# Twelve of 31 convolution taps split between ScalarE and VectorE in a two-layer decoder trunk

## The chip, the cores and the metric

The program runs on one core of a Trainium2 chip. The metric is the device time of one execution in microseconds (us), lower is better. The engines work side by side, each through its own queue in order: TensorE (PE, its weight loads PEld), VectorE (DVE), ScalarE (ACT), GpSimd (POOL) and SyncE (SP), which issues the DMAs here.

## What is computed

Two layers over 256 tokens of width 1024. Each has a gated mixing sublayer of three branches (a convolution module, differential attention, block-sparse attention) that are merged with sigmoid gates and projected by `w_o`, a layer norm, an MLP of width 4096 with squared ReLU, and another layer norm. The part that the change touches is the depthwise causal convolution of 31 taps over 512 channels:

```python
def conv_branch(u, conv_w, conv_b, ln_g, ln_b, w_out):
    a, gt = jnp.split(u, 2, axis=-1)
    h = a * jax.nn.sigmoid(gt)
    h = lax.conv_general_dilated(h, conv_w, window_strides=(1,), padding=[(30, 0)],
        dimension_numbers=("NWC", "WIO", "NWC"), feature_group_count=512) + conv_b
    h = jax.nn.silu(layer_norm(h, ln_g, ln_b))
    return h @ w_out

def reference(x, ...):
    for l in range(2):
        u = x @ w_in[l]
        u_conv, dq, dk, dv, mq, mk, mv, g = jnp.split(u, offs, axis=-1)
        y_a = conv_branch(u_conv, ...)
        y_b = diff_attention(dq, dk, dv, ...)      # rotary on q and k, two softmaxes, subtracted
        y_c = moba_attention(mq, mk, mv, ...)      # rotary on q and k, causal softmax
        gates = jax.nn.sigmoid(g + b_gate[l]).reshape(B, S, 3, D)
        m = gates[:, :, 0] * y_a + gates[:, :, 1] * y_b + gates[:, :, 2] * y_c
        x = layer_norm(alpha * x + m @ w_o[l], ...)
        h = jnp.square(jax.nn.relu(x @ w_ff1[l] + b_ff1[l]))
        x = layer_norm(alpha * x + h @ w_ff2[l] + b_ff2[l], ...)
    return x
```

## The kernel before

**Precision and weights.** Every large matmul is made of three (`mm3`, line 400): the operands are split into a rounded high half and a low half, and high times high, low times high and high times low are added in PSUM. `Weights.get` (line 348) fetches a unit of 128x1024 by DMA into `raw` (a ring of four), ScalarE casts the high half `whi`, VectorE subtracts to get the low half `wlo`; both halves have rings of eight. `split` (line 390) does the same for activations.

**Order of the work.** Nothing is issued where it is written. `Plan.record` (line 111) collects all operations with their dependences. `Plan.latest` (line 185) goes backwards through them and gives each a latest start. `Plan.order` (line 239) then walks forward with a cost for each operation and, on each engine, takes among the operations that are ready the one whose latest start is earliest; a tile whose ring has no free buffer isn't ready. The result fixes the order in each engine's queue; the chip runs each queue in that order. So an operation without an early due time goes where its engine has nothing more urgent that is ready, and a change in one place can reorder the queues elsewhere.

**The convolution.** The gated projection is transposed into `hpad`, four channel groups of 128 channels (partitions) by 30 zeros and 256 tokens (lines 596 to 635). `tap(c, k)` (line 600) is one instruction of VectorE over 128x256: for k = 0 it writes `acc[:, c]` as product plus bias, for k > 0 it adds `hpad` shifted by k, times the tap's weight, one number a partition, to `acc[:, c]`. All 124 taps of a layer are on VectorE (lines 636 to 640); `R.bias` shifts their due time by `CONV_BIAS`, which is 0. `acc` is read much later, by the transposes of `conv_ln` (line 825) while the third set of gates is computed.

**Around it.** TensorE goes on with the two value projections (line 643), the q and k projections with `rope` (lines 657 and 816), which writes each rotated unit into a tile `qk` from a ring of seven, and the attention, whose steps are hung on a counter of weight units (`tick`, line 590): `attn_scores` (line 674) reads two `qk` tiles on TensorE, then VectorE and ScalarE make the softmax, and `d_a` to `d_d` or `m_a` to `m_c` finish each head. `m_a` (line 772) multiplies the weights of a head by one number a partition on ScalarE with `AF.Copy`. Then come `gates` and `outs` (lines 873 and 888): in `outs` VectorE multiplies the projected branch by its gate, adds it to the sum `macc`, and for the last branch splits the sum into `M`, the operand of the projection by `w_o` (line 926). There, on TensorE, the first high times high matmuls are followed by one with the low half of the first piece of `M`. Layer norm, MLP and the next layer follow.

Of the kernel before, what the change touches and what calls it, by code (L numbers as in the profile page):

```python
# [9 lines left out]
F32 = mybir.dt.float32  # L10
F32R = mybir.dt.float32r
AF = mybir.ActivationFunctionType
ALU = mybir.AluOpType

P = 128
D = 1024
SEQ = 256
# [3 lines left out]
TAPS = 31  # L21
# [3 lines left out]
RAWS = 4  # L25
WARM = 5
NW = 8
CONV_BIAS = 0
GATED = (("gate", 0), ("out", 0), ("gate", 1), ("gate", 2), ("out", 1), ("out", 2))
BANKS = {"pm": 2, "pa": 4, "pt": 2}  # L30

# [2 lines left out]
C_CW = 24  # L34
# [332 lines left out]
def kernel(ctx: ExitStack, tc: tile.TileContext, x, xT, w_in, w_p2, w_o, w_f1, w_f2,  # L367
# [7 lines left out]
    work = ctx.enter_context(tc.tile_pool(name="work", bufs=2))  # L375
# [3 lines left out]
    R = Plan(nc)  # L379
# [4 lines left out]
    def slot(dtype=F32R, name="b"):  # L384
        return R.tile(big, [P, 1024], dtype, "big", NSLOT)
# [79 lines left out]
    for (c0, _), (c1, _) in zip(pieces, pieces[1:]):  # L465
        k, n = c0 // 256 % 2, (c1 - c0) // 256
# [11 lines left out]
    for l in range(L):  # L478
        c = R.tile(const, [P, NCOL], F32, f"cols{l}", 1)
# [3 lines left out]
    for t in range(NT):  # L483
        a = slot(F32, "xtok")
# [48 lines left out]
    for l in range(L):  # L533
# [17 lines left out]
        half = R.tile(const, [P, NCOL], F32, f"half{l}", 1)  # L551
# [25 lines left out]
        def qkunit():  # L577
            ps = bank()
            for c in range(2):
                w = W.get(k=KT)  # L580
                for kt in range(KT):
                    mm3(ps[:, c * 256:(c + 1) * 256], at(w, ALLP, kt), x_at(X, kt), kt == 0,
                        kt == KT - 1)
                tick()
            return ps
# [10 lines left out]
        hpad = R.tile(work, [P, 4, TAPS - 1 + SEQ], F32, "hpad", 1)  # L596
        acc = slot(F32, "acc").rearrange("p (c n) -> p c n", c=4)
        R.Pool.memset(hpad[:, :, 0:TAPS - 1], 0.0)

        def tap(c, k):  # L600
            wcol = half[:, C_CW + c * TAPS + k:C_CW + c * TAPS + k + 1]
            src = hpad[:, c, k:k + SEQ]
            if k == 0:
                R.DVE.tensor_scalar(acc[:, c], src, wcol, C[:, C_CB + c:C_CB + c + 1],
                                        op0=ALU.mult, op1=ALU.add)
            else:
                R.DVE.scalar_tensor_tensor(acc[:, c], in0=src, scalar=wcol, in1=acc[:, c],
                                               op0=ALU.mult, op1=ALU.add)
# [25 lines left out]
            o = TAPS - 1 + t * P  # L634
            R.Activation.copy(hpad[:, :, o:o + P], ps.rearrange("p (c n) -> p c n", c=4))
        for c in range(4):
            for k in range(TAPS):
                R.bias = CONV_BIAS
                tap(c, k)
                R.bias = 0.0  # L640


        wv = [W.get(k=2) for _ in range(8)]
# [13 lines left out]
        def rope(ps, dst):  # L657
            qq = R.tile(work, [P, 1024], F32, "zz", 3)
            q, qr = qq[:, :512], qq[:, 512:]
            p3 = ps.rearrange("p (c n) -> p c n", c=2)  # L660
            q3 = q.rearrange("p (c n) -> p c n", c=2)
            qr3 = qr.rearrange("p (c n) -> p c n", c=2)
            d3 = dst.rearrange("p (c n) -> p c n", c=2)
            cb = cosT.rearrange("p (o n) -> p o n", o=1).broadcast_to([P, 2, SEQ])
            R.DVE.tensor_mul(q3, p3, cb)
            for c in range(2):
                R.DVE.tensor_mul(qr3[:, c], p3[:, 1 - c], sinT)
            R.DVE.tensor_sub(d3[:, 0], q3[:, 0], qr3[:, 0])
            R.DVE.tensor_add(d3[:, 1], q3[:, 1], qr3[:, 1])
# [146 lines left out]
        for b in range(2):  # L816
            for u in range(2):
                for w in 'qk':
                    ps = qkunit()
                    d = R.tile(work, [P, 512], F32, "qk", 7)  # L820
                    rope(ps, d)
                    QK[b, w, u] = d.rearrange("p (c n) -> p c n", c=2)

# [136 lines left out]
        for t in range(NT):  # L960
            for c in range(2):
                n, nk = ((512, 2), (256, 4))[c]
# [147 lines left out]
```

## Time and profile before

| | us |
|---|---|
| median of 3 executions (852.14 to 853.23) | 852.98 |
| the profiled execution | 854.34 |
| its span, first to last instruction | 852.6 |
| TensorE busy | 836.9 (98%) |
| VectorE busy | 656.9 (77%) |
| ScalarE busy | 509.0 (60%) |
| mean granted TensorE clock | 0.995 |

How to read it: "busy" is the time in which at least one instruction of the engine is under way; instructions of one engine overlap at their ends, so the mean time of one is longer than the distance between two. A wait is the idle time of an engine ahead of an instruction, with the work that ended it in brackets. Nearly all rows carry line 125, where the planner records every operation, so rows are told apart by the tiles they write and read: `big` is the ring of 16 large buffers (`acc`, gates, sums, `M` and others), `pm`, `pa`, `pt` are PSUM banks, `whi` and `wlo` the weight halves. The granted clock is the share of TensorE's full 2.4 GHz; its lower level is 1.2 GHz, 0.50.

### The profile page before, as it was taken

Reading aid. Unit: us, or ns where it says so; the run is one execution under the profiler, and the core shown is the slowest. Engines: PE = TensorE matmul, PEld = TensorE weight load, DVE = VectorE, ACT = ScalarE, POOL = GpSimd, SP = SyncE. Lnnn points to the kernel's source line nnn. Section 1 sums busy time; section 2 is a strip of 40 time slices with the busy share of each in tenths; the row PEclk is TensorE's granted clock in tenths of the full one; section 3 lists DMA queues with packets and bytes.
Section 4 is the critical chain, followed back from the end, with each engine's and each line's share of the span. In section 5 each row is a group of like instructions: output and inputs, shape, how many; then the busy total and the mean of one; then the engine's idle time right before and its main releaser. Section 6 shows DMA issues by size and latency. Waiting matters only on the chain.

```text
span 852.6 us, 13403 instructions
## 1 busy us (share of the span) xinstructions
PE 836.9 (98%) x5066; PEld 735.4 (86%) x5066; DVE 656.9 (77%) x1155; ACT 509.0 (60%) x852; POOL 18.7 (2%) x26
## 2 busy tenths in 40 slices
PE   9999999999899999999999999999999999999996
PEld 7899989889788888888887999898898888888884
DVE  6799899999896755555688899989988875555545
ACT  6555688557457666556454456976572686656550
POOL 0000100000000000000000000000100000000000
PEclk9999999999999999999999999999999999999998
DMA  9874534436737855555365755334465786556511
GB/s 333 288 255 150 179 100 130 140 120 205 271 122 247 298 185 188 195 191 185 101 196 171 247 164 181 97 128 140 164 206 182 221 295 211 189 195 197 194 54 50
DMA packets 44416, 156.97 MB, mean 184 GB/s; under 512 B 4928, under 2 KB 5696, under 8 KB 44352
## 3 DMA queue, kind: packets, MB, share of 16 engines
q1 hardware_dynamic: 43920, 155.60, 55.0%
q8 instruction: 39, 0.64, 0.3%
q10 hardware_dynamic: 432, 0.52, 0.2%
q14 instruction: 25, 0.20, 0.1%
HBM read 155.06 MB, written 1.05 MB: 183 GB/s over the span
## 4 chain that ended last, share of the span: by engine, by line
PE 93%; DMA 2%; DVE 2%; ACT 1%; issue 0%; DVEq 0%; ACTq 0%
PE pm L125 52%; PE pa L125 29%; PE pt L125 12%; DMA raw<-in_w_f_dram 1%; DVE wlo L125 1%; DVE big L125 1%; ACT whi L125 1%; DMA raw<-in_w_in_dram 1%; DMA zz<-in_xT_dram 0%; ACT zz L125 0%; DVE st L125 0%; DVE zz L125 0%; DVEq L1106 0%; ACT big L125 0%; DVE col L125 0%
## 5 line engine op out<-in xcount | busy, mean ns | idle before, releaser
L125 DVE TENSOR_TENSOR wlo<-raw,whi 128x1024 fp32r<-128x1024 f32 (+1 forms) x282 | 340.5, 1215 | 135.1 <-ACT whi L125 133.1
L125 ACT CAST whi<-raw 128x1024 fp32r<-128x1024 f32 (+1 forms) x282 | 293.3, 1047 | 174.0 <-PE pm L125 57.1
L125 PE MATMUL pm<-big,whi 128*128 128x256 f32 (+1 forms) x1488 | 317.5, 329 | 0.0
L125 PEld LDWEIGHTS pm<-big,whi 128*128 128x128 f32 x1488 | 248.5, 190 | 22.5 <-DVE big L125 0.7
L125 PE MATMUL pa<-whi,big 128*128 128x512 f32 x704 | 219.5, 393 | 3.7 <-DVE big L125 3.4
L125 PE MATMUL pm<-big,wlo 128*128 128x256 f32 x1040 | 209.2, 283 | 0.0
L125 PEld LDWEIGHTS pm<-big,wlo 128*128 128x128 f32 x1040 | 166.5, 191 | 5.9
L125 PEld LDWEIGHTS pa<-whi,big 128*128 128x128 f32 x704 | 131.0, 189 | 30.8 <-DVE big L125 4.2
L125 PE MATMUL pa<-wlo,big 128*128 128x512 f32 x352 | 136.9, 392 | 0.0
L125 DVE SCALAR_TENSOR_TENSOR big<-hpad,half,big 128x256 f32<-128x256 f32 x240 | 102.6, 479 | 0.1
L125 PE MATMUL pm<-whi,big 128*128 128x512 f32 (+1 forms) x320 | 91.3, 370 | 0.0
L125 PEld LDWEIGHTS pa<-wlo,big 128*128 128x128 f32 x352 | 66.5, 189 | 13.9
L125 PEld LDWEIGHTS pm<-whi,big 128*128 128x128 f32 x320 | 58.1, 189 | 10.5 <-ACT zz L125 0.4
L125 PE MATMUL pm<-wlo,big 128*128 128x512 f32 (+1 forms) x160 | 59.1, 371 | 0.0
L125 ACT ACTIVATE zz<-zz 128x512 f32<-128x512 f32 x58 | 36.6, 632 | 31.9 <-DVE zz L125 31.7
L125 PE MATMUL pt<-big,whi 128*128 128x512 f32 x208 | 52.4, 392 | 0.0
L125 ACT ACTIVATE pr<-pr,col 128x256 f32<-128x256 f32 (+1 forms) x96 | 40.1, 446 | 6.9 <-DVE col L125 6.7
L125 PEld LDWEIGHTS pt<-big,whi 128*128 128x128 f32 x208 | 37.4, 189 | 6.6
L125 ACT ACTIVATE big<-pm,cols 128x256 f32<-128x256 f32 x48 | 22.8, 475 | 33.7 <-PE pm L125 33.4
L125 POOL TENSOR_TENSOR col<-col,mhalf 128x1 f32<-128x1 f32 (+1 forms) x20 | 18.1, 905 | 759.8 <-DVE col L125 759.8
L125 DVE TENSOR_TENSOR big<-zz,big 128x512 fp32r<-128x512 f32 (+1 forms) x37 | 25.0, 677 | 12.0 <-ACT big L125 12.0
L125 PEld LDWEIGHTS pm<-wlo,big 128*128 128x128 f32 x160 | 30.2, 188 | 4.8
(83 smaller groups left out, 560.6 us busy)
## 6 DMA issues: line engine op xcount, KB each, us to landing
raw<-in_w_f_dram SPq DMA_DIRECT2D x128, 512.0 KB, 4.3
raw<-in_w_in_dram SPq DMA_DIRECT2D x110, 512.0 KB, 4.2
raw<-in_w_p_dram SPq DMA_DIRECT2D x24, 512.0 KB, 3.4
raw<-in_w_o_dram SPq DMA_DIRECT2D x16, 512.0 KB, 3.8
big<-in_rows_dram SPq DMA_DIRECT2D x10, 512.0 KB, 6.2
raw<-in_w_in_dram SPq DMA_DIRECT2D x4, 256.0 KB, 4.9
big<-in_x_dram SPq DMA_DIRECT2D x2, 512.0 KB, 7.5
out_dram<-big SPq DMA_DIRECT2D x4, 256.0 KB, 2.0
```

What stands on the lines that cost most here:

```text
L125: op.fn = lambda: fn(*args, **kw)
```

## The change

`CONV_BIAS` goes, and so do the two lines that set and reset the bias. Taps 0 of all four channel groups come first, as before. Then, for taps 1 to 12 and for each pair of channel groups, ScalarE writes two products (128x256 each, the tap's weight as a per-partition scale) into the two halves of a tile `tap` from a ring of two, and one VectorE instruction adds both halves, 128x512, to the two groups of `acc`. Taps 13 to 30 stay on VectorE as they were. To make room for the `tap` tiles (2 x 2 KB a partition) the ring of `qk` shrinks from seven tiles of 2 KB to five.

```diff
-CONV_BIAS = 0
+WIDE_TAPS = 12
...
         for c in range(4):
-            for k in range(TAPS):
-                R.bias = CONV_BIAS
+            tap(c, 0)
+        for k in range(1, 1 + WIDE_TAPS):
+            for c2 in range(2):
+                t = R.tile(work, [P, 2, SEQ], F32, "tap", 2)
+                for c in range(2):
+                    n = C_CW + (2 * c2 + c) * TAPS + k
+                    R.Activation.activation(t[:, c], hpad[:, 2 * c2 + c, k:k + SEQ], AF.Copy,
+                                         scale=half[:, n:n + 1])
+                a = acc[:, 2 * c2:2 * c2 + 2]
+                R.DVE.tensor_add(a, a, t)
+        for c in range(4):
+            for k in range(1 + WIDE_TAPS, TAPS):
                 tap(c, k)
-                R.bias = 0.0
...
-                    d = R.tile(work, [P, 512], F32, "qk", 7)
+                    d = R.tile(work, [P, 512], F32, "qk", 5)
```

## Rows read from the trace of the kernel before

**Rows 1.** The page, busy time by engine and the granted clock in 40 slices.

```profile
PE 836.9 (98%) x5066; PEld 735.4 (86%) x5066; DVE 656.9 (77%) x1155; ACT 509.0 (60%) x852; POOL 18.7 (2%) x26
...
PEclk9999999999999999999999999999999999999998
```

**Rows 2.** The chain of waits: start us, us, what.

```profile
87.82 1.52 PE pa L125 x32
...
198.62 17.29 PE pm L125 x144
...
222.56 16.89 PE pa L125 x66
...
288.16 5.47 PE pa L125 x24
```

**Rows 3.** Stretches: length, then busy us (instructions) of PE, PEld, DVE, ACT, POOL; clock, DMA.

```profile
60.00:220.00 160.00, 159.71 (x1229) 147.68 (x1227) 150.02 (x342) 106.34 (x226) 5.22 (x7) 1.00 0.47 153
100.00:130.00 30.00, 30.00 (x214) 26.73 (x213) 28.32 (x76) 26.02 (x72) 3.19 (x3) 1.00 0.46 147
455.00:465.00 10.00, 10.00 (x46) 8.27 (x45) 9.76 (x25) 2.58 (x5) 0.00 (x0) 1.00 0.30 97
```

**Rows 4.** Timeline of TensorE: start, us, what [idle before, ended by], start of both projections.

```profile
222.56 0.50 PE L125 MATMUL pa<-whi,big 128*128 128x512 f32 x1 [2.85 <-DVE big L125]
...
642.46 0.50 PE L125 MATMUL pa<-whi,big 128*128 128x512 f32 x1 [0.51 <-DVE big L125]
```

**Rows 5.** Stretches as in rows 3, just behind the two waits of rows 4.

```profile
223.00:227.00 4.00, 4.00 (x12) 3.10 (x11) 4.00 (x6) 2.17 (x3) 0.00 (x0) 0.57 0.71 256
643.00:647.00 4.00, 4.00 (x19) 3.29 (x18) 4.00 (x7) 1.69 (x2) 0.00 (x0) 1.00 1.00 318
```

**Rows 6.** Timeline of VectorE ahead of the first layer's wait.

```profile
210.18 0.69 DVE L125 SCALAR_TENSOR_TENSOR big<-big,pm 128x512 f32<-128x512 f32 x1 [0.94 <-PE pm L125]
...
215.94 0.69 DVE L125 SCALAR_TENSOR_TENSOR big<-big,pm 128x512 f32<-128x512 f32 x1 [0.46 <-PE pm L125]
...
218.28 1.29 DVE L125 TENSOR_TENSOR big<-big,big 128x512 f32<-128x512 f32 x2
219.48 0.68 DVE L125 SCALAR_TENSOR_TENSOR big<-big,pm 128x512 f32<-128x512 f32 x1
220.08 0.68 DVE L125 TENSOR_TENSOR big<-big,big 128x512 f32<-128x512 f32 x1
220.68 1.22 DVE L125 TENSOR_TENSOR wlo<-raw,whi 128x1024 fp32r<-128x1024 f32 x1
221.82 0.69 DVE L125 SCALAR_TENSOR_TENSOR big<-big,big 128x512 fp32r<-128x512 f32 x1
```

**Rows 7.** Groups by shape, whole span: count, busy us, mean ns of one, idle before.

```profile
L125 DVE SCALAR_TENSOR_TENSOR big<-hpad,half,big 128x256 f32<-128x256 f32 x240 | 102.6, 479 | 0.1
...
L125 DVE TENSOR_TENSOR big<-big,big 128x512 f32<-128x512 f32 x16 | 10.8, 685 | 0.0
```

**Rows 8.** Timelines of VectorE and of ScalarE, instructions of one kind in a row.

```profile
167.95 2.06 DVE L125 SCALAR_TENSOR_TENSOR big<-hpad,half,big 128x256 f32<-128x256 f32 x5
...
140.73 2.19 ACT L125 ACTIVATE pr<-pr,col 128x128 f32<-128x128 f32 x6
```

**Rows 9.** Groups by shape on ScalarE from 140.7 to 142.8 us, columns as in rows 7.

```profile
L125 ACT ACTIVATE pr<-pr,col 128x256 f32<-128x256 f32 x3 | 1.5, 494 | 0.0
L125 ACT ACTIVATE pr<-pr,col 128x128 f32<-128x128 f32 x3 | 1.2, 393 | 0.0
```

**Rows 10.** Stretches, only instructions that touch `hpad`: DVE, ACT, POOL.

```profile
30.00:102.00 72.00, 12.75 (x30) 1.00 (x2) 0.00 (x0) 1.00 0.61 198
...
100.00:130.00 30.00, 10.88 (x25) 0.00 (x0) 0.00 (x0) 1.00 0.46 147
455.00:465.00 10.00, 9.31 (x24) 0.17 (x1) 0.00 (x0) 1.00 0.30 97
```

**Rows 11.** Timeline of VectorE where the first layer's eighth `qk` tile is written.

```profile
105.74 1.09 DVE L125 TENSOR_TENSOR qk<-zz 128x256 f32<-128x256 f32 x3
```

## Prediction

> **What bounds the kernel now.** I read the page's busy times first. TensorE is busy 98% of the span at full granted clock, VectorE 77%, ScalarE 60% [rows 1]. A busy TensorE need not run at its peak, so the chain of waits comes next: it is TensorE almost throughout, and its pieces give the pace, 17.29/144 = 0.120 us for a 256-column matmul and 5.47/24 = 0.228 us for a 512-column one [rows 2]. From 60 to 220 us, where the convolution and the attention of the first layer lie, TensorE is busy 159.71 of 160 us; VectorE, with 150.02, is nearly as full, ScalarE has 106.34 [rows 3]. So almost nothing that VectorE does there reaches the end of the program. The exception is the place where the mixing stage ends and the output projection begins. There the timeline shows TensorE idle for 2.85 us in the first layer and 0.51 us in the second, both ended by VectorE [rows 4]. After the longer wait the granted clock is 0.57 on average over 4 us, between its two levels of 1.2 and 2.4 GHz; after the shorter one it stays at 1.00, 2.4 GHz [rows 5]. The loss by the clock is (1 - 0.57) x 4 = 1.7 us. Together 2.85 + 1.7 + 0.51 = 5.06 us of the span hang on VectorE at these two places; that is all a lighter VectorE can give back. The other idle time of TensorE (852.6 - 836.9 = 15.7 us in all, less the 3.4 us of the two waits) lies at the start, the end and other joints, where the change has no instruction.
>
> **Why VectorE is late there.** The timeline of VectorE shows what the missing low half (the piece at 221.82 us that ends TensorE's wait) stands behind: two additions, one gate product, one more addition and one weight split, from 218.28 to 221.82 us, 3.54 us [rows 6]. The additions are left over from earlier units of the same stage. The planner issues by due time, so work that VectorE could not place among the taps has piled up at the end.
>
> **The change, part by part.** For each layer 12 taps of 4 channel groups, 48 tap instructions, leave VectorE. One lasts 479 ns [rows 7], but neighbours overlap: five stand in 2.06 us, so one costs (2.06 - 0.48)/4 = 0.395 us of the engine [rows 8]. Removed: 48 x 0.395 = 18.96 us. Added: 24 additions of 128x512 from SBUF. Their nearest row is the same operation at the same shape, 685 ns [rows 7], and two in a row stand in 1.29 us, so one costs 1.29 - 0.68 = 0.61 us [rows 6]: 24 x 0.61 = 14.6. VectorE is relieved by 4.3 us a layer. (By whole durations it would be 23.0 - 16.4 = 6.6; the spacing is what an engine that is rarely idle pays, so I take 4.3.)
>
> ScalarE gets 48 products of 128x256 with a per-partition scale. The same form occurs in the normalisation of the attention weights: six of them, half of 256 and half of 128 columns, stand in 2.19 us [rows 8], where 494 and 393 ns each would add up to 2.66 [rows 9]; so neighbours overlap by about 0.09 and a product costs 0.40 us. Added: 19.2 us a layer. From 60 to 220 us ScalarE has 160 - 106.34 = 53.7 us idle, so the load fits on average, and its casts run ahead of TensorE by a ring of eight weight buffers; I cost it at nothing on TensorE's path. But it doesn't fit everywhere: from 100 to 130 us ScalarE is busy 26.02 of 30 [rows 3].
>
> The Trainium skill ("ScalarE: Activation LUTs", Rules for kernel authors) speaks against the move: multiplication belongs on VectorE, which it calls up to about three times faster per element in bf16. The trace doesn't agree for this fp32 shape, 0.40 against 0.395 us [rows 8]. At three times the price the 48 products would be 57.6 us, more than the idle time above.
>
> **New waits.** An addition waits for two products, and a product for a free buffer of two, that is for the addition before the last. Behind a waiting addition stand weight splits and the attention's VectorE work; behind a waiting product the weight casts. The planner foresees both, but a tap is what fills VectorE between urgent pieces, and the filler now depends on ScalarE. A pair of products takes 0.80 us where VectorE took 0.79 for the two taps, so where taps stand in a row VectorE now waits a quarter of the time. In the second layer, 24 of them stand between 455 and 465 us in 9.31 us, with ScalarE busy only 2.58 [rows 3, 10]: 20 taps (7.9 us) become 10 additions, 6.1 us of work and 1.8 us of waiting. In the first layer 30 pieces lie scattered from 30 to 102 us [rows 10]; most stand alone, so a product is ready, and I put the waiting at 1.0 us, about half of the other. They leave 26 slots after the four first taps; I estimate that 16 to 18 of the 24 additions are done by 100 us, two more have their products ready, and 4 to 6 need 8 to 12 products, 3.2 to 4.8 us, in a stretch with 4.0 us of idle ScalarE: another 0.7 us. These three are estimates; their bounds are 0 and the price of the second rival. Net relief: 4.3 - 1.7 = 2.6 us in the first layer, 4.3 - 1.8 = 2.5 in the second.
>
> The first taps stay as they are. The order of summation changes from channel by channel to tap by tap, with no cost of its own; the two removed bias lines were zero. **The ring of five:** the eighth piece of the ring, written at 105.74 us, now needs the third, whose last readers are the score matmuls that begin at 87.82 us and last 1.52 [rows 2, 11]. That is 16.4 us of room, so it costs nothing. If the scores came that much later, rotary work on VectorE would wait and hold up the queue behind it. DMAs are not moved, except that raw buffers come free somewhat earlier.
>
> **Sum.** The first layer's wait of 2.85 shrinks by 2.6 to about 0.25, and a wait below 0.51 left the clock alone [rows 4, 5], so the 1.7 us of low clock go too. The second layer's 0.51 goes. 2.6 + 1.7 + 0.5 = 4.8 us. The profiled execution took 854.34 us, 1.7 around its span of 852.6; it would take 849.5. It lies 1.36 above the median of 852.98, so the median becomes 848.2. Late next is nothing in the mixing stage but TensorE.
>
> **Rivals.** (1) No change. VectorE waited for TensorE twice shortly before the stall, 0.94 us at 210.18 and 0.46 at 215.94 [rows 6]; so it was not behind by load when the last units came, and the order in its queue alone holds the piece back. If the planner keeps additions and a weight split ahead of it, the relief only lengthens those two waits. Time: 853.0, within 1 us. Against it: the leftover additions belong to earlier units and would have been done in the freed time.
> (2) Slower, by ScalarE's crowded stretch. From 100 to 130 us VectorE did 10.88 us of taps [rows 10]; with 30 - 26.02 = 4.0 us of idle ScalarE there are 10 products, 5 additions, 3.1 us. If at least a dozen additions are still open at 100 us, 10.88 - 3.1 = 7.8 us of filler is lost, 3.5 more than was relieved, and the wait grows to 6.4: 853.0 + 3.5 = 856.5. It decides from the point where the lost filler passes 4.3 us a layer. For it: the narrow taps can't start before the last addition. Against it: ScalarE has gaps from 30 to 100 us and little is open by then.
> (3) Half. The relief takes only an addition or two (0.6 to 1.2 us) from ahead of the piece and the low clock remains or shortens: 852.98 - 1.2 - 0.5 = 851.3 down to 849.8 with the clock restored; 850.5.
>
> **How the numbers follow.** Forecast 848.2, own range 847.0 to 849.7 (all of the 5.06 and the spread between executions, or 1.5 less): 0.47. Rival (3) 0.15, (1) 0.23, (2) 0.15. For 8 in 10 the range takes in (1), (3) and the nearer part of (2): 846.9 to 855.5. A measurement of this kernel can tell about 0.2%, 1.7 us, from no change; faster than 851.3 is the forecast and most of (3), 0.60; same 0.23; slower 0.17.
>
> **What would show it.** Right: at the start of both output projections TensorE's idle time is below 0.6 us with the granted clock at 1.00 just behind it, the low half stands behind at most two pieces of VectorE, VectorE's busy time falls by 8 to 10 us in all, ScalarE's rises by about 38. Wrong: additions that wait for the tap buffer on ScalarE for more than 4 us a layer, casts that come late enough for TensorE to wait for them, or a wait of 2 us or more at either projection.

## The result and the profile after

The changed kernel takes 857.99 us in the median of four executions (856.68 to 859.24) against 853.11 for the kernel before on the same chip: ratio 1.0057, 95% interval 1.0044 to 1.007. It is slower by 4.9 us; 848.2 was forecast, and 857.99 lies above the range. The profiled executions stand closer, 856.68 (span 854.6) against 854.34 (852.6): that of the changed kernel is its shortest, with a mean clock of 0.998 against 0.993 to 0.995 in the other three, and that of the kernel before is longer than its median. The last section comes back to that.

The page of the changed kernel, beside [rows 1]:

```profile
PE 836.8 (98%) x5066; PEld 733.8 (86%) x5066; DVE 648.6 (76%) x1107; ACT 545.3 (64%) x948; POOL 17.0 (2%) x26
...
PEclk9999999999999999999999999999999999999999
```

The amounts of work are the forecast ones. VectorE lost 656.9 - 648.6 = 8.3 us of busy time (8 to 10 forecast); ScalarE gained 36.3 us for 96 products, 0.378 us each (38 forecast). So the time isn't in the amount of work. Where it is, the starts of TensorE's pieces tell. Its timeline at the waits between 183 us and the second output projection, in the changed kernel (start, us, what [idle before, ended by]):

```profile
184.90 1.22 PE L125 MATMUL pm<-big,wlo 128*128 128x256 f32 x8 [0.40 <-DVE wlo L125]
...
189.93 1.62 PE L125 MATMUL pa<-cst,big 128*128 128x128 f32 x8 [0.77 <-DVE big L125]
191.45 2.11 PE L125 MATMUL pm<-big,whi 128*128 128x512 f32 x8
...
225.29 0.50 PE L125 MATMUL pa<-whi,big 128*128 128x512 f32 x1 [2.84 <-DVE big L125]
...
644.24 0.50 PE L125 MATMUL pa<-whi,big 128*128 128x512 f32 x1 [1.59 <-DVE big L125]
```

The same three pieces around 190 us in the kernel before, where nothing waits:

```profile
187.16 1.12 PE L125 MATMUL pm<-big,wlo 128*128 128x256 f32 x8
188.12 1.04 PE L125 MATMUL pa<-cst,big 128*128 128x128 f32 x8
188.91 2.09 PE L125 MATMUL pm<-big,whi 128*128 128x512 f32 x8
```

Two things hold TensorE up. At 184.90 us it waits for a weight half, and the pieces behind that start 0.8 us later than before (187.95 against 187.16). Then come the eight transposes of `conv_ln`, the readers of `acc`. They start at 189.93 instead of 188.12 and stand 1.62 us instead of 1.04, since the last taps are still under way on VectorE, until 191.07 us:

```profile
187.82 3.25 DVE L125 SCALAR_TENSOR_TENSOR big<-hpad,half,big 128x256 f32<-128x256 f32 x8
```

The matmuls behind the transposes start at 191.45 instead of 188.91: 2.54 us are lost by here, where the kernel before lost nothing. The first projection's wait is as before, 2.84 against 2.85, though TensorE now arrives 2.7 us later and starts it at 225.29 instead of 222.56. The second wait grew from 0.51 to 1.59 [rows 4]. Between the two, the profiled execution had no low clock behind the first wait (1.00 from 225 to 229 us and from 226 to 230, against 0.57 in [rows 5]). That gives back about 1.6 us: behind the first half of the projection TensorE is only 1.10 us late, at the first transposes of the layer norm (the kernel before, then the change):

```profile
239.29 0.60 PE L125 MATMUL pt<-cst,big 128*128 128x128 f32 x4
240.39 0.60 PE L125 MATMUL pt<-cst,big 128*128 128x128 f32 x4
```

At the same mean clock of 0.998 the change's 856.68 us stands 4.0 to 4.4 above the four executions of the kernel before that are named in the last section (on another chip). The 2.73 us of delay at the first projection and the 1.08 by which the second wait grew are 3.8 of that. What is left of the 4.9 us between the medians isn't assigned.

Why VectorE is late at 190 us shows in the stretches of the changed kernel (length, then busy us and instructions of PE, PEld, DVE, ACT, POOL; clock, DMA share, GB/s):

```profile
30.00:100.00 70.00, 70.00 (x543) 65.83 (x542) 63.81 (x132) 53.86 (x108) 0.70 (x1) 1.00 0.60 196
100.00:130.00 30.00, 30.00 (x214) 26.71 (x214) 21.67 (x56) 27.81 (x80) 3.30 (x3) 1.00 0.41 138
530.00:560.00 30.00, 30.00 (x243) 26.43 (x241) 24.71 (x68) 28.26 (x79) 1.38 (x2) 1.00 0.36 115
```

and of the kernel before:

```profile
30.00:100.00 70.00, 70.00 (x543) 65.82 (x541) 64.99 (x141) 40.76 (x73) 0.73 (x1) 1.00 0.60 196
...
530.00:560.00 30.00, 30.00 (x246) 26.79 (x245) 27.69 (x84) 26.91 (x72) 1.58 (x2) 1.00 0.38 124
```

From 100 to 130 us VectorE is busy 21.67 us where it was busy 28.32 [rows 3]: 6.65 us of the fullest engine beside TensorE are lost in the attention of the first layer, and 2.98 in that of the second. ScalarE is busy 27.81, only 1.8 more than before. TensorE goes on at 30.00 of 30; the loss is paid 60 us later. What became of the taps shows in the stretches of the instructions that touch `tap` (busy us and instructions of DVE, the additions, and of ACT, the products):

```profile
30.00:100.00 70.00, 10.11 (x15) 15.63 (x34) 1.00 0.60 196
100.00:130.00 30.00, 4.81 (x7) 5.02 (x11) 1.00 0.41 138
130.00:160.00 30.00, 1.39 (x2) 1.51 (x4) 1.00 0.34 113
```

Fifteen of the 24 additions are done at 100 us, and products for two more are made (34 of 48). Nine additions are open; seven of them are done by 130 us and the last only at 137.85. The narrow taps of two groups stand behind the additions of their pair, since all go into the same `acc` in program order; the first runs at 134.38 us. From 100 to 130 us [rows 10] has 25 taps, 10.88 us; the changed kernel has no narrow one there. VectorE's timeline there:

```profile
118.73 0.17 DVE L125 TENSOR_SCALAR col<-col 128x2 f32<-128x2 f32 x1 [0.67 <-ACT o L125]
119.76 0.16 DVE L125 TENSOR_TENSOR col<-col,col 128x2 f32<-128x2 f32 x1 [0.87 <-POOL col L125]
121.04 0.42 DVE L125 TENSOR_TENSOR big<-big,pm 128x256 f32<-128x256 f32 x1 [1.12 <-ACT big L125]
...
123.73 0.42 DVE L125 TENSOR_TENSOR big<-big,pm 128x256 f32<-128x256 f32 x1 [2.13 <-ACT big L125]
...
126.71 1.23 DVE L125 TENSOR_TENSOR wlo<-raw,whi 128x1024 fp32r<-128x1024 f32 x1 [1.15 <-ACT whi L125]
```

Hardly any of the idle time is ended by a product: 0.6 us from 100 to 130 us. VectorE waits for the attention's ordinary partners, waits that were there before and were filled with taps. That is why the waits for `tap` look small in the trace while the missing filler costs 6.65 us. So far it is an argument that the filler is missing because the products come late; e9_early tests it.

### The profile page after: what moved, and what is told of

Read it like the earlier page. It is cut to its first block, busy times and chain, and to the rows that moved or that the text cites. A ratio compares the mean times of both kernels' runs of the same rounds, so it can differ in the third digit from the quotient of the medians.

```text
span 854.6 us, 13482 instructions
## 1 busy us (share of the span) xinstructions
PE 836.8 (98%) x5066; PEld 733.8 (86%) x5066; DVE 648.6 (76%) x1107; ACT 545.3 (64%) x948; POOL 17.0 (2%) x26
## 4 chain that ended last, share of the span: by engine, by line
PE 91%; DVE 5%; DMA 2%; ACT 1%; issue 0%; DVEq 0%; ACTq 0%
PE pm L125 50%; PE pa L125 29%; PE pt L125 12%; DVE big L125 3%; DVE wlo L125 2%; DMA raw<-in_w_f_dram 1%; ACT whi L125 1%; DMA raw<-in_w_in_dram 1%; DMA zz<-in_xT_dram 0%; ACT zz L125 0%; ACT big L125 0%; DVE st L125 0%; DVE zz L125 0%; DVEq L1115 0%; DVE col L125 0%
## 5 line engine op out<-in xcount | busy, mean ns | idle before, releaser
L125 DVE SCALAR_TENSOR_TENSOR big<-hpad,half,big 128x256 f32<-128x256 f32 x144 | 61.4, 479 | 0.1
L125 ACT ACTIVATE tap<-hpad,half 128x256 f32<-128x256 f32 x96 | 44.0, 505 | 1.4 <-DVE big L125 1.3
L125 DVE TENSOR_TENSOR big<-big,tap 128x512 f32<-128x512 f32 x48 | 32.8, 687 | 3.0 <-ACT tap L125 2.7
```

The source lines that it names most:

```text
L125: op.fn = lambda: fn(*args, **kw)
```

## The experiments

The theories. **A:** the additions starve, because ScalarE makes their products after its casts and attention work, and the narrow taps stand locked behind them; VectorE has nothing to fill its gaps with. **B:** ScalarE's load as such (its casts come late). **C:** the relief never mattered, the order of VectorE's queue makes the wait at the projection. Later: **D**, two `tap` buffers are too few; **E**, any dependence in the crowded stretch costs all of it; **F**, VectorE's own room before 100 us decides how many additions are open there. Ratios are to the kernel before on the same chip, whose medians were 853.0 to 854.1.

| run | edit | median us | ratio, 95% interval |
|---|---|---|---|
| | the change | 857.99 | 1.0057, 1.0044 to 1.007 |
| e1_no_products | no products | 849.02 | 0.994, 0.9923 to 0.9956 |
| e2_products_only | products without use | 854.15 | 1.0, 0.9986 to 1.0013 |
| e3_wide_last | split taps last | 848.25 | 0.9929, 0.9913 to 0.9944 |
| e4_wide7 | seven split taps, first | 852.84 | 0.9977, 0.9964 to 0.999 |
| e5_ring3 | three `tap` buffers | 856.21 | 1.0027, 1.0013 to 1.0041 |
| e6_mixed | split taps spread | 854.54 | 1.0003, 0.9988 to 1.0018 |
| e7_last16 | sixteen, last | 854.3 | 1.0002, 0.9988 to 1.0016 |
| e8_last8 | eight, last | 849.48 | 0.9942, 0.9923 to 0.9961 |
| e9_early | products due earlier | 849.27 | 0.9951, 0.9934 to 0.9968 |

**Additions without products.** Against the changed kernel (what is added is zero):

```diff
+        still = R.tile(work, [P, 2, SEQ], F32, "tap", 2)
+        R.DVE.memset(still, 0.0)
...
-                t = R.tile(work, [P, 2, SEQ], F32, "tap", 2)
-                for c in range(2):
-                    n = C_CW + (2 * c2 + c) * TAPS + k
-                    R.Activation.activation(t[:, c], hpad[:, 2 * c2 + c, k:k + SEQ], AF.Copy,
-                                         scale=half[:, n:n + 1])
...
-                R.DVE.tensor_add(a, a, t)
+                R.DVE.tensor_add(a, a, still)
```

> The 24 additions a layer read a tile of zeros that is written once; the products on ScalarE, and with them the part of taps 1 to 12 in the sum, are left out. It has VectorE's relief of 4.3 us a layer without ScalarE's load and without the new wait. Theory A (the additions starve: they wait for products in ScalarE's crowded stretch, and the narrow taps are locked behind them): 848.2, the waits of TensorE at both output projections below 0.6 us, as the prediction had it. Theory B (ScalarE's load itself, which delays its casts and the attention): also about 848. Theory C (the relief never mattered, the wait at the projection comes from the order of VectorE's queue): 853, the first layer's wait again near 2.9 us.

849.02 us. The relief of VectorE is worth 5.1 us when nothing starves; neither projection has a wait left, and VectorE is busy 28.41 us from 100 to 130 us. So the sum of the prediction (2.85 + 1.7 + 0.51, of which 4.8 were to be had) stands, the relief does reach the end, and C falls as it was put; what is right in it comes in the next section. Seventeen of the 24 additions run before 100 us here, though none of them ever waits, and seven after.

**Products without additions.** Against the kernel before: the products are made into the ring of two and read by nobody, all 31 taps stay on VectorE, the `qk` ring is five.

```diff
+        for k in range(1, 13):
+            for c2 in range(2):
+                t = R.tile(work, [P, 2, SEQ], F32, "tap", 2)
+                for c in range(2):
+                    n = C_CW + (2 * c2 + c) * TAPS + k
+                    R.Activation.activation(t[:, c], hpad[:, 2 * c2 + c, k:k + SEQ], AF.Copy,
+                                         scale=half[:, n:n + 1])
...
-                    d = R.tile(work, [P, 512], F32, "qk", 7)
+                    d = R.tile(work, [P, 512], F32, "qk", 5)
```

> All 31 taps stay on VectorE as before; the 48 products a layer are made on ScalarE into the ring of two and read by nobody, and the ring of qk is five. It has ScalarE's load and the shorter ring without the wait of an addition. Theory A: 853, no difference that can be measured, VectorE's busy time from 100 to 130 us near 28.3 again. Theory B: 856 or more. Theory C: 853.

854.15, ratio 1.0, with the waits of the kernel before at both projections. The load on ScalarE and the ring of five cost nothing that can be measured. B falls, with one reservation: here all 48 products of the first layer ran before 100 us, 58.86 us of ScalarE from 30 to 100 us against 40.76 in the kernel before; the load in the crowded stretch is the subject of e9_early.

**The split taps last.** The same work; only the order of the taps changes.

```diff
-        for k in range(1, 1 + WIDE_TAPS):
+        for c in range(4):
+            for k in range(1, TAPS - WIDE_TAPS):
+                tap(c, k)
+        for k in range(TAPS - WIDE_TAPS, TAPS):
...
-        for c in range(4):
-            for k in range(1 + WIDE_TAPS, TAPS):
-                tap(c, k)
```

> The same instructions as the changed kernel, but the twelve split taps are 19 to 30 and come last; the narrow taps 1 to 18 come first. So narrow taps fill VectorE in ScalarE's crowded stretch and the additions fall behind it, where ScalarE has room. Theory A: faster than before, 848 to 850, VectorE's busy time from 100 to 130 us back at 28, first layer's wait below 1 us. Theory B: about 857, as ScalarE's load is the same. Theory C: 853 to 858 with the first layer's wait near 2.9 us.

848.25, 0.9929: faster than both kernels, with the waits gone that the change was forecast to remove. Its stretches of the instructions that touch `hpad` (narrow taps on DVE; on ACT the products and what fills `hpad`), then of all instructions:

```profile
100.00:130.00 30.00, 11.73 (x28) 0.00 (x0) 0.00 (x0) 1.00 0.43 144
130.00:160.00 30.00, 8.17 (x19) 5.08 (x12) 0.00 (x0) 1.00 0.36 114
160.00:190.00 30.00, 0.00 (x0) 14.63 (x33) 0.20 (x1) 1.00 0.56 185
...
100.00:130.00 30.00, 30.00 (x215) 26.84 (x214) 28.44 (x77) 25.91 (x71) 3.20 (x3) 1.00 0.43 144
```

The attention's gaps are filled with narrow taps that wait for nobody, and the products fall where ScalarE was idle: in the kernel before it was busy 16.49 of the 30 us from 160 to 190. TensorE waits at neither projection.

**Fewer split taps, in the old place** (`WIDE_TAPS = 7` instead of 12).

> Seven split taps at the front instead of twelve: 14 additions a layer. The changed kernel had finished 15 of 24 by 100 us, so here hardly any is open when ScalarE's crowded stretch begins. Theory A: VectorE's busy time from 100 to 130 us near 28, time 851 to 853: a relief of 2.5 us a layer, less the waiting at the front. Theory B: 853 plus seven twelfths of 4.9, 855.9. Theory C: 853 to 858.

852.84, 0.9977: a gain of 1.3 us. All 14 additions are done by 100 us, VectorE is busy 28.11 us from 100 to 130 us, nothing is lost there; with 24 additions the loss was 6.65. The small relief leaves a wait of 2.25 us at the first projection and 0.51 at the second.

**Three buffers.**

```diff
-                t = R.tile(work, [P, 2, SEQ], F32, "tap", 2)
+                t = R.tile(work, [P, 2, SEQ], F32, "tap", 3)
...
-                    d = R.tile(work, [P, 512], F32, "qk", 5)
+                    d = R.tile(work, [P, 512], F32, "qk", 4)
```

> The changed kernel with three tap buffers instead of two; the room comes from the q and k ring, which shrinks from five tiles to four. Nothing is left out. Theory A (the products come late because ScalarE does the weight casts and the attention ahead of them, and the narrow taps stand behind): a third buffer lets at most one more pair be made ahead, worth one addition and two taps at 100 us, about 1.4 us of the 6.65 that VectorE loses from 100 to 130 us: 855 to 858, VectorE's busy time from 100 to 130 us 26.5 to 28. Rival D (two buffers are too few: products wait for the addition before the last): the additions are done by 100 us, 848 to 852, VectorE 28 or more in that stretch. If the ring of four holds up the rotary work, the wait is on VectorE's qk pieces near 100 to 110 us and the time may be above 858.

856.21, 1.0027: still slower than before, so a third buffer isn't the cure that D makes it. (The shorter `qk` ring that pays for it was not run by itself; that two buffers are enough, e9_early shows.) VectorE is busy only 21.21 us from 100 to 130 us, less even than with two buffers; the forecast of 26.5 to 28 for it was wrong, while the time fell where A said. The gain over the change is in the second layer, whose projection no longer waits. In the first layer three additions at 112.30 us empty all three buffers, and ScalarE still makes no product between these two rows of its timeline:

```profile
111.64 0.50 ACT L125 ACTIVATE tap<-hpad,half 128x256 f32<-128x256 f32 x1
...
126.80 0.53 ACT L125 ACTIVATE tap<-hpad,half 128x256 f32<-128x256 f32 x1
```

**The split taps spread over the thirty.**

```diff
-        for k in range(1, 1 + WIDE_TAPS):
+        wide = [1 + (i * 30) // WIDE_TAPS for i in range(WIDE_TAPS)]
+        for k in range(1, TAPS):
+            if k not in wide:
+                for c in range(4):
+                    tap(c, k)
+                continue
...
-        for c in range(4):
-            for k in range(1 + WIDE_TAPS, TAPS):
-                tap(c, k)
```

> The changed kernel with the twelve split taps spread evenly over the thirty (every second or third) instead of standing first; the narrow taps go tap by tap over the four groups. Nothing is left out. Theory A: the split taps that fall between 100 and 130 us still starve, but there are fewer of them (about 12 x 30/100, 4 of 12, instead of the 9 additions and all that stood behind them), so about a third to a half of the harm is left: 850 to 854, VectorE 27 to 28.2 us from 100 to 130 us. Rival E (only the number of additions that are open when the crowded stretch begins counts, and any dependence there costs the whole stretch): as the changed kernel, 856 to 859. Theory B (ScalarE's load as such): as the changed kernel, 856 to 858.

854.54, 1.0003, half a microsecond above the upper end that A gave, and below the 856 to 859 of its rivals B and E. Four additions fall between 100 and 130 us; VectorE is busy 25.76 us, less than the 27 to 28.2 that A gave: 2.6 us lost instead of 6.65. From 130 to 160 us another 1.5 go (26.18 against 27.69 in the kernel before), and with these 4.1 us the relief of 4.3 is used up.

**More and fewer, last** (`WIDE_TAPS = 16` and 8 in the version with the split taps last).

> The version with the split taps last, with sixteen of them instead of twelve. Nothing is left out. Theory A has a bound here: the waits at the projections are already gone with twelve, so the further relief (1.4 us a layer) is worth nothing, while 16 more products, 6.4 us, must find room on ScalarE before the layer norm of the branch reads the sum at about 189 us, where with twelve ScalarE is busy 28.7 of 30 us. The narrow taps end some 6 us earlier, where ScalarE still has 5.9 of 30 us idle. If they fit, 848 to 849.5; if not, the layer norm's transposes on TensorE wait for the sum, 850 to 855. A rival that says only the relief counts (the more taps leave VectorE, the faster): 847 or less.

> The version with the split taps last, with eight of them instead of twelve. Nothing is left out. Theory A: VectorE is relieved by 4.3 x 8/12 = 2.9 us a layer and nothing starves; the 2.85 us wait of the first projection nearly goes, the 0.51 of the second goes, the low clock behind the first mostly goes: 848.5 to 850.5. A rival that the place alone matters and any relief beyond one or two additions is idle: 848 as with twelve. A rival that the gain comes in proportion to the relief alone (5.9 us x 8/12): 850.

Sixteen take 854.3, eight 849.48, twelve 848.25. With sixteen the additions begin before 130 us and fall into the later part of the attention: from 130 to 160 us VectorE is busy 27.06 and ScalarE 27.56, against 27.95 and 24.15 with twelve, and from 160 to 190 us VectorE has 26.26 against 27.95. The waits return, 1.58 us at the first projection and 2.19 at the second, not at the layer norm, where A had put them. More relief isn't more gain. Eight leave 0.56 us at the first projection and none at the second. Their time fits A; it doesn't exclude a gain in plain proportion to the relief, 850, since the interval reaches 850.2.

**Products made early.** The change with nothing but the products' due time moved:

```diff
+                    R.bias = -40000.0
                     R.Activation.activation(t[:, c], hpad[:, 2 * c2 + c, k:k + SEQ], AF.Copy,
                                          scale=half[:, n:n + 1])
+                    R.bias = 0.0
```

> The changed kernel with the due time of the products alone moved forward by 40 us, so that ScalarE makes each as soon as a tap buffer is free, ahead of its casts and its attention work; the additions and all else keep their due times. Nothing is left out. Theory A in its form 'order' (ScalarE has the time for the products and only makes them too late): additions always find their products, VectorE's busy time from 100 to 130 us is back at 28 us or more, the waits of TensorE at 185 to 190 us go, 848 to 853. Theory A in its form 'capacity' (from 100 to 130 us ScalarE, busy 26.0 of 30 us before the change, can't hold them): the attention's casts and softmax come late instead, TensorE or VectorE waits for those, 855 to 859. Rival F (VectorE's own room before 100 us sets how many additions are done by then, whatever ScalarE does): still about 15 of 24 done at 100 us; if F and 'order' both hold, the rest is done by some 115 us rather than 138.

849.27, 0.9951, with the split taps in the place that the change gave them. The instructions that touch `tap`, then all instructions, in this kernel:

```profile
30.00:100.00 70.00, 10.14 (x15) 15.72 (x34) 1.00 0.60 196
100.00:115.00 15.00, 3.88 (x6) 3.65 (x8) 1.00 0.60 188
115.00:130.00 15.00, 2.35 (x4) 2.67 (x6) 1.00 0.21 69
...
100.00:130.00 30.00, 30.00 (x215) 26.74 (x214) 27.98 (x74) 27.78 (x82) 3.09 (x3) 1.00 0.40 128
```

This settles order against capacity. At 100 us the state is that of the change: 15 additions done. F holds, ScalarE made no difference before that. ScalarE's busy time from 100 to 130 us is also that of the change, 27.78 against 27.81: "capacity" falls. Only the order on ScalarE differs: the last addition starts at 118.22 us instead of 137.85, narrow taps run from 117.49, and VectorE has 27.98 us of work instead of 21.67. TensorE doesn't wait at 185 to 190 us, nor at the second projection; 1.59 us stay at the first.

## Why the prediction was wrong

**What there was to win: right in size.** The two projections hang on VectorE, and with the relief and without starving they lose their waits: 5.1 us in e1_no_products, 5.9 in e3_wide_last, against 4.8 forecast. The 5.9 lies above the 5.06 that the prediction called all there was to give back; its interval is 4.8 to 7.4.

**How the relief works: by order, where the prediction had load.** It let the first wait shrink microsecond by microsecond with VectorE's load. The rows show steps. Here are the last gate product for which VectorE itself waits for TensorE, and the first low half, which TensorE then waits for, in the changed kernel (in the kernel before they start at 215.94 and 221.82 [rows 6]):

```profile
218.67 0.69 DVE L125 SCALAR_TENSOR_TENSOR big<-big,pm 128x512 f32<-128x512 f32 x1 [0.46 <-PE pm L125]
...
224.55 0.68 DVE L125 SCALAR_TENSOR_TENSOR big<-big,big 128x512 fp32r<-128x512 f32 x1
```

In e3_wide_last the first low half stands ahead of that product, and is done before TensorE begins the projection at 218.19 us:

```profile
216.77 0.69 DVE L125 SCALAR_TENSOR_TENSOR big<-big,big 128x512 fp32r<-128x512 f32 x1
...
218.39 0.69 DVE L125 SCALAR_TENSOR_TENSOR big<-big,pm 128x512 f32<-128x512 f32 x1 [0.32 <-PE pm L125]
```

In the kernel before, the change, e2_products_only, e5_ring3 and e6_mixed the distance is 5.88 or 5.89 us, with the same pieces in the same order between, and the wait is 2.84 or 2.85 us in all five, however late TensorE comes. In the kernels that keep more of the relief the queue has another order, with whole pieces less in that distance: one addition in e4_wide7 (wait 2.25), an addition and a weight split in e7_last16 and e9_early (1.58 and 1.59). So the first rival, chance 0.23, had this mechanism right, that the order in the queue holds the piece back. Its condition, that the planner keeps this order under the relief, did not hold in them.

**The prices: right.** A product adds 0.378 us of busy time, against 0.40; VectorE is lighter by 8.3 us against twice 4.3. The factor of up to about three for VectorE that the Trainium skill gives ("ScalarE: Activation LUTs", Rules for kernel authors) is one for bf16, which no run here has; for this fp32 shape it doesn't show, 0.378 us on ScalarE beside 0.395 for VectorE's whole tap.

**Cover on ScalarE and the ring of five: right.** e2_products_only, ratio 1.0.

**Waiting from 30 to 100 us: about right.** VectorE lost 64.99 - 63.81 = 1.2 us against 1.0, but with 15 additions done, one to three fewer than estimated.

**Waiting from 100 to 130 us: the step that failed.** It was put at 0.7 us; the loss there is 6.65. Three things were wrong in it. Nine additions were open, seven of them without products, where six to eight and four to six were estimated. ScalarE's 4.0 us of idle time were taken as time for products; but ScalarE takes its work by due time, the products' due time is late, as the sum is read only at 190 us, and it put them behind the attention: none between the pair at 109.49 and the single one at 121.28 us. And the wait was priced as the time that an addition waits, while what is lost is all the filler behind it: the 18 narrow taps of each group, which were the reserve for exactly this stretch. "The planner foresees both" was no protection: the order that it chose starves VectorE.

**The second rival named this mechanism, at a chance of 0.15.** Its arithmetic came out in part by luck: its 7.8 us of lost filler were all from 100 to 130 us with a dozen additions open; measured are 6.65 there with nine open, and 1.2 before. Less the relief of 4.3 that leaves its 3.5 us of delay. Counted to 222 us it is less (columns as above, the kernel before first):

```profile
30.00:222.00 192.00, 189.71 (x1399) 174.12 (x1396) 179.50 (x386) 126.51 (x248) 5.22 (x7) 1.00 0.52 169
30.00:222.00 192.00, 190.84 (x1397) 173.83 (x1396) 172.24 (x360) 141.70 (x293) 5.30 (x7) 1.00 0.51 166
```

VectorE has done 7.26 us less, of which 4.15 (half of the 8.3) are work that it no longer has. The 3.1 us left are still to do, and TensorE begins the first projection 2.73 us later than before. The rival had the place wrong: it let the projection's wait grow to 6.4 us, while the delay was paid by 191 us, at the transposes of `conv_ln` and just ahead of them, and the wait stayed 2.84. Its "against" (ScalarE has gaps from 30 to 100 us, so little is open by then) looked at the wrong engine: until 100 us it is VectorE that has no room. Its slots there were in [rows 10]: 12.75 us less the four first taps at 0.395 leave 11.2, or 18 additions of 0.61 if none ever waits, and e1_no_products had 17. So six open additions were the least to reckon with.

**The second layer: too hopeful.** 1.8 us of waiting were estimated for the burst alone; the stretch from 530 to 560 us, the same attention, lost 2.98 more. But that sum doesn't give the wait: e6_mixed lost the same 2.98 there (24.71 against 27.69) and kept the 0.51. What made it 1.59 is again a piece in the queue, a weight split between the last product and the low half, in the kernel before and in the change:

```profile
641.12 0.68 DVE L125 SCALAR_TENSOR_TENSOR big<-big,pm 128x512 f32<-128x512 f32 x1
641.72 0.69 DVE L125 SCALAR_TENSOR_TENSOR big<-big,big 128x512 fp32r<-128x512 f32 x1
```

```profile
641.76 0.69 DVE L125 SCALAR_TENSOR_TENSOR big<-big,pm 128x512 f32<-128x512 f32 x1 [0.34 <-PE pm L125]
642.37 1.22 DVE L125 TENSOR_TENSOR wlo<-raw,whi 128x1024 fp32r<-128x1024 f32 x1
643.50 0.69 DVE L125 SCALAR_TENSOR_TENSOR big<-big,big 128x512 fp32r<-128x512 f32 x1
```

**The clock term** of 1.7 us was right in size, about 1.6 by the trace of the change, but it doesn't belong to the wait in every execution (last section). A slip without weight: the lower end of the third rival, 849.8, is 849.6 by its own terms.

Open: why the planner puts that weight split there in the change and not in e6_mixed. No run varied the order at the end of the stage by itself.

## What to carry to other kernels

Work that an engine does in the gaps of other work is worth its independence: before making it depend on another engine, find the stretch that uses it as filler, and price the whole reserve behind the first waiting piece, not that piece's wait. Idle time of the other engine counts only if its order will put the new work into it; ask who goes first there. With the same instructions, the order alone made 857.99, 854.54, 849.27 or 848.25 us: put the dependent part last, where the partner is idle, or make the partner's share due early. And where an engine waits for one piece in another's queue, count the pieces ahead of it: here the wait changed by whole pieces.

## What the hardware showed unexpectedly

The same wait of TensorE is followed by a low clock in one execution and not in another. The stretch from 223 to 227 us, behind a first wait of 2.84 or 2.85 us, in e2_products_only and in e6_mixed (columns as above):

```profile
223.00:227.00 4.00, 4.00 (x12) 3.17 (x11) 4.00 (x6) 1.68 (x3) 0.00 (x0) 0.57 0.83 282
```

```profile
223.00:227.00 4.00, 4.00 (x19) 3.29 (x18) 4.00 (x6) 1.87 (x3) 0.00 (x0) 1.00 0.82 284
```

0.57, as in [rows 5], with 12 matmuls begun in 4 us, and 1.00 with 19. In e5_ring3 it is 0.57 again, from 226.5 to 230.5 us behind 2.84 us; in the change it is 1.00. A shorter wait shows both as well: behind 2.25 us in e4_wide7 the clock is 0.59 from 222 to 226 us, behind 2.19 us at the second projection of e7_last16 it is 1.00 from 643 to 647. The times of one kernel go with the clock, with exceptions: of the 25 executions of the kernel before on one chip, the four with a mean clock of 0.998 took 852.3 to 852.7 us and the three longest, 855.5 to 855.8, had 0.994, but a fourth with 0.994 took 852.8. e1_no_products, which has no such wait, stayed between 848.8 and 849.8 at 0.997 to 0.998. Whether the spread is narrower without the wait isn't shown by four executions; four of the kernel before spread no further, 852.14 to 853.33. But one profiled execution, with the low clock or without, can stand more than a microsecond off its median: the change's did by 1.3, and e6_mixed's by 1.8.
